# A transformer block on one core: q and k of three heads from unnormalised x, head 0's v and gate by seven products

## The chip, the cores and the metric

The kernel runs on one core of a Trainium2 chip. Five engines work beside each other, each through its own instructions in order: TensorE (PE; its weight loads are shown as PEld), VectorE (DVE), ScalarE (ACT), GpSimd (POOL) and SyncE (SP). DMAs are issued from a queue of SP, ACT or POOL. The metric is the time of one execution on the device in microseconds (us); smaller is better.

## The reference, cut to what matters

One encoder layer for 512 tokens of width 1024, in float32. The columns of `w_in` are [conv x | conv B | conv C | q | k | v | swish gate | gate A | gate R].

```python
def rmsnorm(x, g):
    xf = x.astype(jnp.float32)
    y = xf * lax.rsqrt(jnp.mean(xf * xf, axis=-1, keepdims=True) + EPS)
    return (y * g.astype(jnp.float32)).astype(x.dtype)
...
        h = rmsnorm(x, g_mix[l])
        proj = h @ w_in[l]
        xc, gb, gc, q, k, v, g_sw, gate_a, gate_r = jnp.split(proj, split_points, axis=-1)
...
        qf = rotary(q.reshape(b, s, RET_HEADS, RET_QK_DIM).astype(jnp.float32)) * (RET_QK_DIM ** -0.5)
        kf = rotary(k.reshape(b, s, RET_HEADS, RET_QK_DIM).astype(jnp.float32))
        vf = v.reshape(b, s, RET_HEADS, RET_V_DIM).astype(jnp.float32)
...
        ret_f = retention_chunkwise(qf, kf, vf, lg_f, strict=False)
        ret_b = jnp.flip(retention_chunkwise(jnp.flip(qf, 2), jnp.flip(kf, 2), jnp.flip(vf, 2),
                                             lg_b, strict=True), 2)
...
        y_r = (ret.astype(dt) * jax.nn.silu(g_sw)) @ w_r_out[l]
        merged = jax.nn.sigmoid(gate_a) * y_a + jax.nn.sigmoid(gate_r) * y_r
        x = x + merged @ w_o[l]
        h2 = rmsnorm(x, g_ffn[l])
        x = x + (jax.nn.silu(h2 @ w_ff_gate[l]) * (h2 @ w_ff_up[l])) @ w_ff_down[l]
    return rmsnorm(x, g_final)
```

There are four heads; q and k of a head are 256 wide, v and its swish gate 512. The retention weight of a pair of tokens is a power of a forward or a backward decay, by their distance.

## The kernel before, in words

**Precision.** Every matmul of the reference is made of three: each operand is split into a rounded part `hi` and a remainder `lo`, and `hi*hi + hi*lo + lo*hi` is summed in a bank (`mm3`, L282 to L286, and the inner loops of `prod`, L325, and `prod_tm`, L369). The split is a cast on ACT (L171, or L174 with a scale) and a subtraction on VectorE (L172 or L175).

**Weights.** A list written out by hand, `plan()`, gives the order in which weights are used. A block ("c") is loaded as 1 MB in two halves (L208) and split. A form of a quad ("q") comes from quarters of a pair of matrices (loaded at L232), some of them summed first on VectorE (L244), and is then split. `take()` hands out the next weights and prepares up to two units (`AHEAD`) more.

**Quads.** `strassen` (L379) makes two products that share their left side by seven half products instead of eight, `a11, s1, s2, a12, s3, a22, s4`, from sums of quarters of the activations (`sums`, L597) and of the weights. Some products add into a bank that a copy on ACT (`snap`, L376) has just read. A quad is 7 x 24 = 168 matmuls of 128x512.

**Start.** Eight small matmuls keep TensorE busy. Then `prefetch(4, load_x, split_x)` loads pieces of the first weight block and of x in turn, all from SP's queue, with the small columns `cols` ahead of x (L431, L432). `split_x` scales x by the gain `g_mix` and splits it into `xu`: this is x without its 1/rms. `SumSq` sums the squares; `rstd_tokens` (L470) gives 1/rms by token (a power on POOL, L482), and `rstd_row` (L490) the same as a row on all partitions, by two matmuls (L493, L494).

**Head 0's v and gate.** They are made first from `xu` by two plain products (`token_major`, L301), 96 matmuls each. Their eviction (L576) multiplies by 1/rms. `rstd_row` is asked for between the two products. Then x is normalised (L587) and split into `xg`, and the sums for the quads follow (L607).

**Order after that.** For each head: the quad of v and gate (not for head 0), then q and k from `xg` (`do_qk`, 96 matmuls of 128x512) with the rotation on VectorE out of the banks. Then two quads for the gates A and R, then the decay tables (`decays`), then the conv mixer, which is the first work after this stage with 256-wide products (L325). Everything is stored to DRAM from POOL's queue (`store`, L566) and loaded again later. The order of instructions on each engine is set when the kernel is built, by a scheduler that takes the program's order as priority and fills gaps with later work that is ready. So the decay tables, last in the program, stand within the first quad on the chip.

**End.** The last two products of the FFN's last part give the output in four blocks of tokens. `ev` adds a block to y (`to_y`, L1087 on VectorE, the square on ACT, L1089), scales and stores the block before it (`put`, L1111 on VectorE, or L1109 on ACT), and forms 1/rms of its own block (`rms`, L1097 and a power on POOL, L1099).

Pools: `big` has 14 tiles of 128x2048, `tmp` 9 of 128x512 (`t512`), `misc` 2, PSUM 8 banks.

Of the kernel before, what the change touches and what calls it, by code (L numbers as in the profile page):

```python
# [17 lines left out]
P = 128  # L18
D = 1024
# [25 lines left out]
AHEAD = 2  # L45
LEAD = 4

WIDTH = {"w": 512, "x": 256, "a": 512, "f": 256, "d": 512}  # L50
# [5 lines left out]
def plan():  # L56
# [16 lines left out]
            for u in (0, 2):  # L73
                out.append(("q", ("w", c0, c1), name, u, 2))

    for c in (C_V, C_G):
        for r in (0, 512):
            b("w_in", r, 4, c, 512)
    for h in range(HEADS):
        if h:  # L80
            quad(C_V + h * VD, C_G + h * VD)
        a("w_in", C_Q + h * QK)
        a("w_in", C_K + h * QK)
    for c in (0, 512):
        quad(C_GA + c, C_GR + c)
    for c0, c1 in ((C_XC, C_GC), (C_XC + 256, C_GC + 256), (C_GB, C_GB + 256)):
# [56 lines left out]
def block_kernel(ctx: ExitStack, tc: tile.TileContext, xT, xtok, wpack, wquad, cols, decs, rot, g_ffn, g_final, out):  # L143
# [284 lines left out]

    def load_x(k, n=1):
        if k == 0:  # L430
            nc.sync.dma_start(cols_sb, cols)  # L431
        nc.sync.dma_start(xs[k // 4][:, k % 4:k % 4 + n, :], xT[:, k:k + n, :])  # L432

    def split_x(k):
        split(xs[k // 4][:, k % 4, :], xu[0][k // 4][:, k % 4, :], xu[1][k // 4][:, k % 4, :],
# [15 lines left out]
    class SumSq:  # L451
# [18 lines left out]
        def rstd_tokens(self):  # L470

            ps = bank()
            for nb in range(NB):
                sl = slice(nb * P, (nb + 1) * P)
                nc.tensor.matmul(ps[:, 2 * nb:2 * nb + 2], self.hi[:, sl], ones_r[:, 0:2], start=True, stop=False)
                nc.tensor.matmul(ps[:, 2 * nb:2 * nb + 2], self.lo[:, sl], ones_r[:, 0:2], start=False, stop=True)
            r = small.tile([P, NB], F32, tag="rtok", name="rtok", bufs=2)
            v = small.tile([P, NB], F32, tag="rtokv", name="rtokv", bufs=2)
            nc.vector.tensor_scalar(
                out=v, in0=ps[:, 0:2 * NB].rearrange("p (n two) -> p n two", two=2)[:, :, 0],  # L480
                scalar1=1.0 / D, scalar2=EPS, op0=ALU.mult, op1=ALU.add)
            nc.gpsimd.tensor_tensor(out=r, in0=v, in1=mhalf[:, 0:NB], op=ALU.pow)  # L482
# [5 lines left out]
            return r  # L488

        def rstd_row(self):  # L490

# [6 lines left out]
    for k in range(8):  # L498
        ss.add(xs[k // 4][:, k % 4, :])
    ss.split()  # L500


    dec = const.tile([P, 8], F32, name="dec")
# [20 lines left out]

    nc.vector.tensor_scalar_mul(lgam[:, 4:8], lgam[:, 4:8], -1.0)


    def decays():
        delta_i = big.tile([P, 896], mybir.dt.int32, tag="big", name="delta_i", padded_shape=[P, 2048])
        nc.gpsimd.iota(delta_i, pattern=[[1, 896]], base=-384, channel_multiplier=-1)  # L530
        delta = big.tile([P, 896], F32, tag="big", name="delta", padded_shape=[P, 2048])
        nc.vector.tensor_copy(delta, delta_i)
        for h in range(HEADS):
            scr = big.tile([P, 896], F32, tag="big", name="scr", padded_shape=[P, 2048])
            tab = misctile(896, "tab")
            nc.vector.tensor_scalar(out=scr, in0=delta, scalar1=0.0, scalar2=lgam[:, 4 + h:5 + h],
                                    op0=ALU.min, op1=ALU.mult)
            nc.vector.tensor_scalar(out=tab, in0=delta, scalar1=0.0, scalar2=lgam[:, h:h + 1],
                                    op0=ALU.max, op1=ALU.mult)
            nc.vector.tensor_tensor(out=scr, in0=scr, in1=tab, op=ALU.add)  # L540
            nc.scalar.activation(tab, scr, AF.Exp)
            nc.sync.dma_start(tabs[h], tab)

    def kept(name):
        return dram.tile([P, 4, 512], F32, name=name)

    tabs = [dram.tile([P, 896], F32, name=f"tab{h}") for h in range(HEADS)]
    qkd = [(kept(f"qh{h}"), kept(f"ql{h}")) for h in range(HEADS)]  # L550
    vd = [kept(f"v{h}") for h in range(HEADS)]
    sgd = [kept(f"sg{h}") for h in range(HEADS)]
    gad = [kept(f"ga{j}") for j in range(2)]
    grd = [kept(f"gr{j}") for j in range(2)]

    zd = [[dram.tile([P, n, 4, 256], F32, name=f"z{i}{n}{j}") for i in range(2)]
          for j, n in enumerate((2, 2, 2, 1))]

    def keep(dst, src):
        hi, lo = t512(F32R), t512(F32R)  # L560
        split(src, hi, lo)
        for d, t in zip(dst, (hi, lo)):
            store(d, t.bitcast(F32))

    def store(dst, t):
        nc.gpsimd.dma_start(dst, t)  # L566


    def before_v(kk):
        if kk == 7:  # L570
            rtok.append(ss.rstd_tokens())
    rtok = []
# [11 lines left out]
    xg = quarters()  # L584
    for k in range(8):
        xk = xs[k // 4][:, k % 4, :]
        nc.vector.scalar_tensor_tensor(out=xk, in0=xk, scalar=gmix[:, k:k + 1], in1=rrow,  # L587
                                       op0=ALU.mult, op1=ALU.mult)
    for i in range(2):
        for k in (0, 2):  # L590
            split(xs[i][:, k:k + 2, :], xg[0][i][:, k:k + 2, :], xg[1][i][:, k:k + 2, :])

    def form_tile():
        t = big.tile([P, 2, 4, 256], F32R, tag="big", name="xform", padded_shape=[P, 2, 4, 256])
        return t[:, 0], t[:, 1]

    def sums(a11, a12, a21, a22):  # L597
        out = {}
        for name, o, in0, in1, op in (
                ("s1", a22, a21, a22, ALU.subtract), ("s3", a21, a11, a21, ALU.subtract),  # L600
                ("s2", a11, a22, a11, ALU.subtract), ("s4", a12, a12, a11, ALU.add)):
            nc.vector.tensor_tensor(out=o, in0=in0, in1=in1, op=op)
            out[name] = form_tile()
            split(o, *out[name])
        return out

    xf = sums(*(xs[i][:, :, o:o + 256] for o in (0, 256) for i in range(2)))  # L607
    for n, i, o in (("a11", 0, 0), ("a12", 1, 0), ("a22", 1, 256)):
        xf[n] = tuple(t[i][:, :, o:o + 256] for t in xg)
    xforms = {n: of(t) for n, t in xf.items()}  # L610

    def do_qk(h):
        for j in range(2):
            pss = []
            feature_major(xg, lambda m, ps: pss.append(ps))
            cos, sin = rcs[:, 0, :], rcs[:, 1, :]
            for i, (c1, c2, op) in enumerate(((cos, sin, ALU.subtract), (sin, cos, ALU.add))):
                a, b = t512(), t512()
                nc.vector.tensor_tensor(out=a, in0=pss[0], in1=c1, op=ALU.mult)
                nc.vector.tensor_tensor(out=b, in0=pss[1], in1=c2, op=ALU.mult)  # L620
                nc.vector.tensor_tensor(out=a, in0=a, in1=b, op=op)
                keep([t[:, 2 * j + i, :] for t in qkd[h]], a)
# [24 lines left out]

    def conv(m, b, u, c):
# [435 lines left out]
    def to_y(ps, nb, half):  # L1084

        yt, ac, i = y[half][:, nb, :], acs[nb], done[nb]
        nc.vector.tensor_tensor(out=yt, in0=ps, in1=yt, op=ALU.add)  # L1087
        sq = t512()
        nc.scalar.activation(sq, yt, AF.Square, accum_out=ac[:, i:i + 1])  # L1089
# [3 lines left out]
        done[nb] += 1  # L1093

    def rms(nb):
        ac = acs[nb]
# [55 lines left out]
def pack_weights(arrays):  # L1152
    out = np.empty((len(BLOCKS), P, CH), np.float32)
    for i, (_, name, row, nk, col, ncol) in enumerate(BLOCKS):
        blk = arrays[name][row:row + nk * P, col:col + ncol]
        out[i] = blk.reshape(nk, P, ncol).transpose(1, 0, 2).reshape(P, CH)
    return out

# [58 lines left out]
```

## Time and profile before

| what | value |
|---|---|
| median of 3 runs | 1043.47 us (1043.3 to 1043.92) |
| the profiled execution's own time | 1043.97 us |
| its span, first to last instruction | 1042.2 us |
| granted TensorE clock | 0.998 |
| VectorE busy / ACT busy / POOL busy | 84% / 50% / 10% of the span |
| DMA | 175.07 MB, mean 168 GB/s |

A line of the timeline reads: start in us from the span's start, duration, engine, line of the kernel, operation, what it writes and reads, shapes, count, and in brackets how long the engine had been idle and what ended that. A line of the chain of work reads: start, duration, engine and line, count. A line of groups gives busy time and the mean of one in ns behind the first bar, and idle time ahead of it behind the second. Starts are the measure for a stream of matmuls, since their ends are modelled and overlap.

### The profile page before, as it was taken

How to read it: one execution, taken by the hardware profiler on the slowest of the kernel's cores; microseconds unless marked ns; L12 is line 12 of the kernel's file. 1: busy time of each engine (PE TensorE's matmuls, PEld its weight loads, DVE VectorE, ACT ScalarE, POOL GpSimd, SP SyncE). 2: the span in 40 equal slices, each digit the busy share in tenths (PEclk: the TensorE clock that was granted, in tenths of full speed). 3: DMA queues.
4: the chain of work that ended last, by engine and by line, in shares of the span. 5: the costliest groups of instructions: out<-in, count | busy, mean ns of one | idle time of the engine just before them, and what ended most of it. 6: DMA issues, size and time to landing. Idle time of an engine off the chain costs nothing.

```text
span 1042.2 us, 14832 instructions
## 1 busy us (share of the span) xinstructions
PE 1028.3 (99%) x5664; PEld 897.0 (86%) x5664; DVE 875.5 (84%) x1127; ACT 523.4 (50%) x698; POOL 107.7 (10%) x180
## 2 busy tenths in 40 slices
PE   8999999999999999999999999999999999999996
PEld 7788888888888998888888888889998999899985
DVE  6999786858787888697989998669998899889995
ACT  6546745452656545243443234355555565556553
POOL 0121111111111004202011000000002000110011
PEclk9999999999999999999999999999999999999999
DMA  9635638173645576919176535630319322663322
GB/s 325 223 117 201 236 123 281 71 254 119 199 141 182 169 284 233 341 42 358 42 283 247 205 111 173 236 113 28 92 45 275 117 85 78 193 152 102 122 35 87
DMA packets 49688, 175.07 MB, mean 168 GB/s; under 512 B 6480, under 2 KB 6480, under 8 KB 46288
## 3 DMA queue, kind: packets, MB, share of 16 engines
q1 hardware_dynamic: 36592, 131.12, 36.9%
q0 software_dynamic: 13024, 43.00, 12.9%
q8 instruction: 44, 0.72, 0.3%
q14 instruction: 28, 0.23, 0.1%
HBM read 135.56 MB, written 38.54 MB: 167 GB/s over the span
## 4 chain that ended last, share of the span: by engine, by line
PE 77%; issue 9%; DVE 7%; DMA 3%; POOL 2%; ACT 1%; SPq 0%; POOLq 0%; DVEq 0%; ACTq 0%
PE bank L369 29%; PE bank L325 27%; PE bank L285 7%; PE bank L284 7%; PE bank L286 7%; DVE wlo L172 1%; POOL z L566 1%; DVE big L185 1%; DMA big<-ql 1%; DMA big<-xT 1%; DMA z<-t 1%; DMA tab<-tab 0%; DVE big L172 0%; DVE t L464 0%; DVE big L175 0%
## 5 line engine op out<-in xcount | busy, mean ns | idle before, releaser
L171 ACT CAST whi<-raw 128x1024 fp32r<-128x1024 f32 (+1 forms) x281 | 288.6, 1032 | 302.7 <-PE bank L369 66.4
L172 DVE TENSOR_TENSOR wlo<-raw,whi 128x1024 fp32r<-128x1024 f32 (+1 forms) x281 | 335.8, 1202 | 108.8 <-ACT whi L171 107.8
L325 PE MATMUL bank<-xform,whi 128*128 128x256 f32 x1440 | 260.3, 283 | 0.0
L325 PEld LDWEIGHTS bank<-xform,whi 128*128 128x128 f32 x1440 | 224.8, 192 | 0.7 <-ACT t L376 0.6
L325 PE MATMUL bank<-xform,wlo 128*128 128x256 f32 x720 | 203.7, 283 | 0.0
L369 PE MATMUL bank<-whi,big 128*128 128x512 f32 x548 | 172.4, 390 | 0.0
L244 DVE TENSOR_TENSOR raw<-raw 128x1024 f32<-128x1024 f32 (+1 forms) x124 | 148.5, 1205 | 1.8 <-DMA raw<-wquad 0.4
L325 PEld LDWEIGHTS bank<-xform,wlo 128*128 128x128 f32 x720 | 138.2, 192 | 0.0
L369 PEld LDWEIGHTS bank<-whi,big 128*128 128x128 f32 x548 | 102.7, 188 | 22.4 <-DVE big L172 0.6
L369 PE MATMUL bank<-wlo,big 128*128 128x512 f32 x274 | 106.7, 389 | 0.0
L369 PE MATMUL bank<-whi,xform 128*128 128x512 f32 x320 | 101.2, 389 | 0.3 <-ACT t L376 0.3
L284 PE MATMUL bank<-whi,big 128*128 128x512 f32 x240 | 94.3, 395 | 1.8 <-ACT big L174 1.8
L285 PE MATMUL bank<-wlo,big 128*128 128x512 f32 x240 | 94.3, 393 | 0.0
L286 PE MATMUL bank<-whi,big 128*128 128x512 f32 x240 | 93.4, 392 | 0.0
L284 PE MATMUL bank<-big,whi 128*128 128x512 f32 x224 | 87.1, 389 | 0.0
L285 PE MATMUL bank<-big,whi 128*128 128x512 f32 x224 | 87.1, 389 | 0.0
L286 PE MATMUL bank<-big,wlo 128*128 128x512 f32 x224 | 87.1, 389 | 0.0
L376 ACT COPY t<-bank 128x512 f32<-128x512 f32 x96 | 55.5, 585 | 35.8 <-PE bank L369 17.2
L369 PEld LDWEIGHTS bank<-whi,xform 128*128 128x128 f32 x320 | 60.1, 188 | 13.1 <-ACT t L376 0.7
L369 PE MATMUL bank<-wlo,xform 128*128 128x512 f32 x160 | 62.2, 389 | 0.0
L369 PEld LDWEIGHTS bank<-wlo,big 128*128 128x128 f32 x274 | 51.4, 188 | 10.5
L284 PEld LDWEIGHTS bank<-whi,big 128*128 128x128 f32 x240 | 45.5, 190 | 12.5 <-ACT big L174 2.1
(173 smaller groups left out, 1398.6 us busy)
## 6 DMA issues: line engine op xcount, KB each, us to landing
raw<-wquad SPq DMA_DIRECT2D x124, 512.0 KB, 4.4
raw<-wpack SPq DMA_DIRECT2D x58, 512.0 KB, 4.9
z<-t POOLq DMA_DIRECT2D x24, 256.0 KB, 4.9
zform<-z POOLq DMA_DIRECT2D x6, 1024.0 KB, 6.2
v<-t POOLq DMA_DIRECT2D x16, 256.0 KB, 5.0
sg<-t POOLq DMA_DIRECT2D x16, 256.0 KB, 3.3
qh<-t POOLq DMA_DIRECT2D x16, 256.0 KB, 2.6
ql<-t POOLq DMA_DIRECT2D x16, 256.0 KB, 2.7
```

What stands on the lines that cost most here:

```text
L171: nc.scalar.copy(hi, src)
L172: nc.vector.tensor_tensor(out=lo, in0=src, in1=hi.bitcast(F32), op=ALU.subtract)
L185: nc.vector.transpose(o[:, :, :, b, :], i[:, :, :, q, :])
L244: nc.vector.tensor_tensor(out=t, in0=t, in1=raws[quad, more, u][:, 0:n], op=ALU.add)
L284: nc.tensor.matmul(ps, lh, rh, start=first, stop=False)
L285: nc.tensor.matmul(ps, lh, rl, start=False, stop=False)
L286: nc.tensor.matmul(ps, ll, rh, start=False, stop=last)
L325: nc.tensor.matmul(o, l[:, c], r[:, k], start=start and s == 0 and k == 0 and i == 0, stop=stop and k == 3 and i == 2, skip_group_check=True)
L369: nc.tensor.matmul(pss[tt], l, r[:, c], start=start and k == 0 and i == 0, stop=stop and k == n - 1 and i == 2, skip_group_check=True)
L376: nc.scalar.copy(t, ps)
L566: nc.gpsimd.dma_start(dst, t)
```

## The change

- `plan()` starts with six blocks, for each of three heads (`EARLY`) the columns of q and k side by side; head 0's v and gate become a quad as the others are.
- The first products are now q and k of heads 0 to 2 from `xu`, 96 matmuls a head, into four banks, which ACT copies into a `big` tile each. `rstd_tokens` goes ahead of step 7 of head 0's product, `rstd_row` ahead of step 1 of head 1's, and the normalisation of x and its splits after it.
- The rotation of these q and k takes a table of cosines and sines that is multiplied by the row of 1/rms (`rcn`). The six rotations are held back, one for each quad (`turn_one`).
- `decays()` makes the tables in two halves of 448 columns, each entry as the product of two exponentials, in `t512` tiles, right after head 0's quad in the program. Their stores go from SP's queue to POOL's.
- x is loaded from ACT's queue, `cols` from POOL's.
- At the end, `put` of the block before is ordered behind the new block's sum on VectorE and behind its square on ACT.

```diff
+EARLY = 3
...
-    for c in (C_V, C_G):
+    for h in range(EARLY):
         for r in (0, 512):
-            b("w_in", r, 4, c, 512)
+            b("w_in", r, 4, (C_Q + h * QK, C_K + h * QK), 512)
     for h in range(HEADS):
-        if h:
-            quad(C_V + h * VD, C_G + h * VD)
-        a("w_in", C_Q + h * QK)
-        a("w_in", C_K + h * QK)
+        quad(C_V + h * VD, C_G + h * VD)
+        if h >= EARLY:
+            a("w_in", C_Q + h * QK)
+            a("w_in", C_K + h * QK)
...
         if k == 0:
-            nc.sync.dma_start(cols_sb, cols)
-        nc.sync.dma_start(xs[k // 4][:, k % 4:k % 4 + n, :], xT[:, k:k + n, :])
+            nc.gpsimd.dma_start(cols_sb, cols)
+        nc.scalar.dma_start(xs[k // 4][:, k % 4:k % 4 + n, :], xT[:, k:k + n, :])
...
+    def decays():
+        for o in (0, 448):
+            delta = t512(mybir.dt.int32)[:, 0:448]
+            nc.gpsimd.iota(delta, pattern=[[1, 448]], base=o - 384, channel_multiplier=-1)
+            ahead, behind = (t512()[:, 0:448] for _ in range(2))
+            nc.vector.tensor_scalar(out=ahead, in0=delta, scalar1=0.0, scalar2=None, op0=ALU.max)
+            nc.vector.tensor_scalar(out=behind, in0=delta, scalar1=0.0, scalar2=None, op0=ALU.min)
+            for h in range(HEADS):
+                f, g = (t512()[:, 0:448] for _ in range(2))
+                nc.scalar.activation(f, ahead, AF.Exp, scale=lgam[:, h:h + 1])
+                nc.scalar.activation(g, behind, AF.Exp, scale=lgam[:, 4 + h:5 + h])
+                nc.vector.tensor_tensor(out=f, in0=f, in1=g, op=ALU.mult)
+                store(tabs[h][:, o:o + 448], f)
...
+    early = []
+    for h in range(EARLY):
+        pss = [bank() for _ in range(4)]
+        for kk in range(8):
+            if kk % 4 == 0:
+                c = Chunk()
+            if (h, kk) == (0, 7):
+                ss.rstd_tokens()
+            if (h, kk) == (1, 1):
+                rrow = snap(ss.rstd_row())
+
+                xg = quarters()
...
+            for m in range(4):
+                mm3(pss[m], c.w(kk % 4, m * P, P), act_pair(xu, kk), kk == 0, kk == 7)
+        t = bigtile()
+        for m in range(4):
+            nc.scalar.copy(t[:, m, :], pss[m])
+        early.append(t)
...
-    for dst, func in ((vd[0], AF.Copy), (sgd[0], AF.Silu)):
-        def ev(nb, ps):
-            t = t512()
-            nc.scalar.activation(t, ps, func, scale=rtok[0][:, nb:nb + 1])
-            store(dst[:, nb, :], t)
-        token_major(xu, 0, 2, ev, None if rtok else before_v)
-        if func == AF.Copy:
-            rrow = snap(ss.rstd_row())
...
+    rcn = misctile(D, "rcn").rearrange("p (i n) -> p i n", i=2)
     for i in range(2):
+        nc.vector.tensor_tensor(out=rcn[:, i, :], in0=rcs[:, i, :], in1=rrow, op=ALU.mult)
+    held = [(h, j) for h in range(EARLY) for j in range(2)]
+
+    def turn_one():
+
+        if held:
+            h, j = held.pop(0)
+            rotate(h, j, early[h][:, 2 * j, :], early[h][:, 2 * j + 1, :], rcn)
...
             store(left[:, 2 + tt, :], t)
+            if tt:
+                turn_one()
...
     for h in range(HEADS):
-        if h:
-            do_quad(vd[h], sgd[h], AF.Silu)
-        do_qk(h)
+        do_quad(vd[h], sgd[h], AF.Silu)
+        if h == 0:
+            decays()
+        if h >= EARLY:
+            do_qk(h)
     for j in range(2):
         do_quad(gad[j], grd[j], AF.Sigmoid, AF.Sigmoid)
-    decays()
+    while held:
+        turn_one()
...
     def ev(ps, nb, half):
-        to_y(ps, nb, half)
+        add, square = to_y(ps, nb, half)
         if held:
-            put(held.pop())
+            with tc.issue_after(add.ins), tc.issue_after(square.ins):
+                put(held.pop())
         else:
             gain(0, 0)
             gain(1, 0)
```

More of the change, by code (lines that the diff above doesn't have):

```diff
@@ new lines, in kept @@
+    def kept(name):
+        return dram.tile([P, 4, 512], F32, name=name)
+    tabs = [dram.tile([P, 896], F32, name=f"tab{h}") for h in range(HEADS)]
+    qkd = [(kept(f"qh{h}"), kept(f"ql{h}")) for h in range(HEADS)]
+    vd = [kept(f"v{h}") for h in range(HEADS)]
+    sgd = [kept(f"sg{h}") for h in range(HEADS)]
+    gad = [kept(f"ga{j}") for j in range(2)]
+    grd = [kept(f"gr{j}") for j in range(2)]
+    zd = [[dram.tile([P, n, 4, 256], F32, name=f"z{i}{n}{j}") for i in range(2)]
+          for j, n in enumerate((2, 2, 2, 1))]
@@ new lines, in keep, with store @@
+    def keep(dst, src):
+        hi, lo = t512(F32R), t512(F32R)
+        split(src, hi, lo)
+        for d, t in zip(dst, (hi, lo)):
+            store(d, t.bitcast(F32))
+    def store(dst, t):
+        nc.gpsimd.dma_start(dst, t)
+    rrow = None
+    early = []
[9 more added lines that the diff above has]
+                xg = quarters()
+                for k in range(8):
+                    xk = xs[k // 4][:, k % 4, :]
+                    nc.vector.scalar_tensor_tensor(out=xk, in0=xk, scalar=gmix[:, k:k + 1], in1=rrow,
+                                                   op0=ALU.mult, op1=ALU.mult)
+                for i in range(2):
+                    for k in (0, 2):
+                        split(xs[i][:, k:k + 2, :], xg[0][i][:, k:k + 2, :], xg[1][i][:, k:k + 2, :])
+            for m in range(4):
[4 more added lines that the diff above has]
+        early.append(t)
@@ new lines, in form_tile, with sums @@
+    def form_tile():
+        t = big.tile([P, 2, 4, 256], F32R, tag="big", name="xform", padded_shape=[P, 2, 4, 256])
+        return t[:, 0], t[:, 1]
+    def sums(a11, a12, a21, a22):
+        out = {}
+        for name, o, in0, in1, op in (
+                ("s1", a22, a21, a22, ALU.subtract), ("s3", a21, a11, a21, ALU.subtract),
+                ("s2", a11, a22, a11, ALU.subtract), ("s4", a12, a12, a11, ALU.add)):
+            nc.vector.tensor_tensor(out=o, in0=in0, in1=in1, op=op)
+            out[name] = form_tile()
+            split(o, *out[name])
+        return out
@@ L503, in block_kernel @@
+    xf = sums(*(xs[i][:, :, o:o + 256] for o in (0, 256) for i in range(2)))
+    for n, i, o in (("a11", 0, 0), ("a12", 1, 0), ("a22", 1, 256)):
+        xf[n] = tuple(t[i][:, :, o:o + 256] for t in xg)
+    xforms = {n: of(t) for n, t in xf.items()}
     dec = const.tile([P, 8], F32, name="dec")
@@ L525, in block_kernel @@
     nc.vector.tensor_scalar_mul(lgam[:, 4:8], lgam[:, 4:8], -1.0)
[L528 to L542, printed above, removed]
@@ L597, in sums @@
[L597 to L607, printed above, removed]
@@ L608, in block_kernel, with rotate @@
-    for n, i, o in (("a11", 0, 0), ("a12", 1, 0), ("a22", 1, 256)):
-        xf[n] = tuple(t[i][:, :, o:o + 256] for t in xg)
-    xforms = {n: of(t) for n, t in xf.items()}
+    def rotate(h, j, t1, t2, table):
+        cos, sin = table[:, 0, :], table[:, 1, :]
+        for i, (c1, c2, op) in enumerate(((cos, sin, ALU.subtract), (sin, cos, ALU.add))):
+            a, b = t512(), t512()
+            nc.vector.tensor_tensor(out=a, in0=t1, in1=c1, op=ALU.mult)
+            nc.vector.tensor_tensor(out=b, in0=t2, in1=c2, op=ALU.mult)
+            nc.vector.tensor_tensor(out=a, in0=a, in1=b, op=op)
+            keep([t[:, 2 * j + i, :] for t in qkd[h]], a)
@@ L615, in do_qk @@
             feature_major(xg, lambda m, ps: pss.append(ps))
[L616 to L622, printed above, removed]
+            rotate(h, j, *pss, rcs)
     def do_quad(left, right, func, func_left=None):
```

40 lines of the change are left out of this document (5 added, 35 removed).

## The prediction

> **What bounds the kernel now.** I read the page first, then what TensorE waited for, then the busy time by stage, then the chain of work and single stretches of the timeline.
>
> ```profile
> span 1042.2 us, 14832 instructions
> ## 1 busy us (share of the span) xinstructions
> PE 1028.3 (99%) x5664; PEld 897.0 (86%) x5664; DVE 875.5 (84%) x1127; ACT 523.4 (50%) x698; POOL 107.7 (10%) x180
> ```
>
> The profiled execution took 1043.97 us for this span, 0.50 over the median of 1043.47. TensorE is busy for 99% of it, so I ask two things of every edit: does it remove matmuls, and does it make TensorE wait. These are its waits in the first 120 us, longest first, and the busy time by stage (the first quad product starts at 78, the last product of the gates ends at 334):
>
> ```profile
> PE bank L284 <- ACT big L174: 1.8, 1, 1.8
> PE bank L493 <- ACT t L171: 1.7, 1, 1.7
> ```
>
> ```profile
> core 0: us, PE busy (x) PEld busy (x) DVE busy (x) ACT busy (x) POOL busy (x), PEclk, DMA share, GB/s
> 0.00:78.00 78.00, 73.34 (x315) 60.16 (x316) 66.08 (x106) 44.08 (x59) 11.02 (x22) 1.00 0.63 221
> 50.00:80.00 30.00, 30.00 (x134) 24.85 (x133) 29.59 (x32) 14.83 (x17) 5.23 (x9) 1.00 0.30 106
> 78.00:334.00 256.00, 255.70 (x1128) 211.38 (x1127) 199.45 (x217) 138.08 (x169) 35.87 (x66) 1.00 0.54 183
> 334.00:1042.00 708.00, 699.28 (x4224) 625.47 (x4222) 610.01 (x805) 341.28 (x471) 60.82 (x92) 1.00 0.47 157
> ```
>
> The reader is to see that from 78 to 334 TensorE lacks 0.3 us of 256, and that VectorE is the second engine. In 50 to 80 it is busy for 29.59 of 30 us and TensorE still loses nothing. The price of a matmul comes from the chain of work, where the two gate quads stand as one piece:
>
> ```profile
> 258.10 76.21 PE bank L369 x336
> ```
>
> 76.21 / 336 = 0.2268 us for one 512-wide matmul, and the last gate quad ends at 334.3.
>
> **Products.** Head 0's v and gate go from two plain products, 2 x 8 x 4 x 3 = 192 matmuls, to seven half products of 2 x 4 x 3 = 24, that is 168. q and k keep 2 x 2 x 8 x 3 = 96 a head in either form. So 24 matmuls go: 24 x 0.2268 = **-5.4 us**. They lie on the engine that is 99% busy, and nothing but a new wait can give them back. Ahead of the first quad stand 192 + 96 = 288 matmuls before and 3 x 96 = 288 after, so the sums and splits of x have the same cover as now.
>
> **The wait for the row of 1/rms.** Before, the row is asked for right after the v product:
>
> ```profile
> 30.41 1.02 POOL L482 TENSOR_TENSOR rtok<-rtokv,mhalf 128x4 f32<-128x4 f32 x1 [5.75 <-DVE lw L517]
> ```
>
> ```profile
> 31.21 0.39 PE L286 MATMUL bank<-whi,big 128*128 128x512 f32 x1
> 33.33 0.50 PE L493 MATMUL bank<-t,ones_r 128*128 128x512 f32 x1 [1.72 <-ACT t L171]
> ```
>
> The two starts are 2.12 us apart where 0.23 would do: 1.9 us lost, plus 0.2 before the second half (a guess). After, the sums still go in ahead of step 7 of the first product, but the row is asked for after step 0 of the next one: 24 matmuls (5.4 us) behind them where there were 12 (2.7 us). The chain was 1.9 late and gets 2.7 more. The decay logarithm, whose small VectorE steps (L517) sit between the links of this chain, now comes later in the program. I take **-2.1**, bounds -2.3 and 0. Next late would be the copying out of the first product's four banks (4 ACT copies of 0.59, row below), which has 12 matmuls of cover; ACT is free for 34 of the first 78 us.
>
> **x on ACT's queue, the columns on POOL's.** The start, first SP's issues, then ACT's instructions, then TensorE:
>
> ```profile
> 0.73 0.39 SPq L208 DMA_DIRECT2D raw<-wpack  x1
> 1.17 0.42 SPq L431 DMA_DIRECT2D cols_sb<-cols  x1
> 1.64 0.42 SPq L432 DMA_DIRECT2D big<-xT  x1
> ...
> 4.48 3.32 SPq L432 DMA_DIRECT2D big<-xT  x3
> ```
>
> ```profile
> 4.18 0.62 ACT L171 CAST whi<-raw 128x512 fp32r<-128x512 f32 x1 [1.86 <-DMA raw<-wpack]
> 5.90 0.72 ACT L174 ACTIVATE big<-big,cols_sb 128x512 fp32r<-128x512 f32 x1 [1.10 <-DMA big<-xT]
> ```
>
> ```profile
> 6.67 0.79 PE L284 MATMUL bank<-whi,big 128*128 128x512 f32 x1 [1.85 <-ACT big L174]
> ```
>
> The first matmul waits for x's first load, issued third. It can go 1.64 - 0.73 = 0.91 us earlier: the best end. Against it, the last three x loads held SP's queue until 7.80. If they hold ACT's queue as long, the cast at 4.18 and the scaling at 5.90 stand behind them: 7.80 + 0.62 + 0.72 = 9.14, 2.5 us later: the worst end. Every matmul follows, so either counts in full. ACT's queue will carry the six x loads alone, without the weight and column loads that SP had in flight, so I take a value near the good end, **-0.2**. The columns go to a POOL that works 11 of 78 us. I price their move at nothing: their cover is x's own landing, and if they land after it the loss lies within the same bounds.
>
> **VectorE and ACT under the quads.** The stage from the first quad to the last now holds six quads and one q/k: 6 x 168 + 96 = 1104 matmuls, 250.3 us. VectorE's prices, from its groups in 78 to 334 and two stretches of its timeline:
>
> ```profile
> L172 DVE TENSOR_TENSOR wlo<-raw,whi 128x1024 fp32r<-128x1024 f32 x81 | 98.9, 1223 | 45.1 <-ACT whi L171 44.8
> L244 DVE TENSOR_TENSOR raw<-raw 128x1024 f32<-128x1024 f32 x38 | 46.2, 1222 | 0.4
> ```
>
> ```profile
> 44.85 4.63 DVE L172 TENSOR_TENSOR big<-big 128x1024 fp32r<-128x1024 f32 x4
> ...
> 71.51 0.68 DVE L619 TENSOR_TENSOR t<-bank,rcs 128x512 f32<-128x512 f32 x1
> 72.11 0.68 DVE L620 TENSOR_TENSOR t<-bank,rcs 128x512 f32<-128x512 f32 x1
> ```
>
> Back to back, a 1024-wide one takes (4.63 - 1.22) / 3 = 1.14, a 512-wide one 72.11 - 71.51 = 0.60. A quad has 14 splits, 8 weight sums and 6 result sums: 22 x 1.14 + 6 x 0.60 = 28.7. With one held rotation (8 x 0.60 = 4.8) it is 33.5 of its 38.1 us. Six make 201. Head 3's q/k adds 4 x 1.14 + 16 x 0.60 = 14.2, the decays 12 x at most 0.60 = 7.2, at 512-wide prices for 448 columns. Together **222.6 of 250.3 us, 89%**, where the stage stood at 199.45 of 256 (78%). It fits, and 50 to 80 shows that 98% can fit, so I price the rotations, the sums and the two products for the normalised table at nothing. Their cover is these 28 us of slack.
>
> ACT carries what can disturb TensorE. After the product s3 its bank is copied out (L376) and the product a22 writes the same bank. The first bank's copy has six matmuls, 1.36 us, of cover. The decays now issue 16 exponentials inside the first quads:
>
> ```profile
> 94.33 0.59 ACT L376 COPY t<-bank 128x512 f32<-128x512 f32 x1 [0.73 <-PE bank L369]
> 94.81 1.05 ACT L171 CAST whi<-raw 128x1024 fp32r<-128x1024 f32 x1
> 95.88 1.28 ACT L541 ACT_TABLE_LOAD   x1
> 97.17 0.96 ACT L541 ACTIVATE tab<-scr 128x896 f32<-128x896 f32 x1
> ```
>
> A table load ahead of such a copy costs TensorE 1.28 + 0.59 - 1.36 = 0.5 us; a load with an exponential behind it 1.47. The bounds are 0 and 4 x 1.47 = 5.9. I take two loads, **+1.0**, because ACT is half idle and its order already leaves room ahead of the copies (idle 0.73 in the first row). The table stores go to POOL, eight instead of SP's four, on an engine busy for 36 of 256 us. What waits behind them are stores of v and gates, which nobody reads before the scores.
>
> **The end.** VectorE's last instructions, and the last matmul:
>
> ```profile
> 1031.17 1.42 DVE L1111 SCALAR_TENSOR_TENSOR big<-big,fin,gf 128x512 f32<-128x512 f32 x2 [0.66 <-POOL fin L1099]
> 1032.50 0.69 DVE L1087 TENSOR_TENSOR big<-bank,big 128x512 f32<-128x512 f32 x1
> 1033.98 0.16 DVE L1097 SCALAR_TENSOR_TENSOR fin<-fin 128x1 f32<-128x1 f32 x1 [0.79 <-ACT t L1089]
> 1034.79 0.75 DVE L1111 SCALAR_TENSOR_TENSOR big<-big,fin,gf 128x512 f32<-128x512 f32 x1 [0.65 <-POOL fin L1099]
> 1035.46 0.68 DVE L1087 TENSOR_TENSOR big<-bank,big 128x512 f32<-128x512 f32 x1
> 1036.93 0.16 DVE L1097 SCALAR_TENSOR_TENSOR fin<-fin 128x1 f32<-128x1 f32 x1 [0.79 <-ACT t L1089]
> 1037.75 0.75 DVE L1111 SCALAR_TENSOR_TENSOR big<-big,fin,gf 128x512 f32<-128x512 f32 x1 [0.66 <-POOL fin L1099]
> ```
>
> ```profile
> 1033.33 0.39 PE L369 MATMUL bank<-whi,big 128*128 128x512 f32 x1
> ```
>
> The last bank is ready at 1033.72, but its sum (L1087) starts at 1035.46, behind the scaling of the block before it. With that scaling ordered behind the sum and behind the square, the sum starts at about 1033.75 and the rest of the chain (2.29 to the last scaling, then the store) follows unchanged: **-1.7**, bounds -1.8 and 0. The sum before it has room too: its bank is full 12 matmuls earlier, at 1031.0, and the pair of scalings then ends by about 1033.1. What is queued behind the new order is the earlier block's scaling. It leaves at about 1035.9 at the latest, still before the last block's.
>
> **Sum**: -5.4 - 2.1 - 0.2 - 1.7 + 1.0 = -8.4 us. Against the profiled execution that is 1043.97 - 8.4 = 1035.6, on the median **1035.1**.
>
> **Rivals.** (1) The x loads hold ACT's queue: +2.5 in place of -0.2, 1037.8. For it: the 3.32 us row. Against it: a queue of its own. (2) The copies come late in the first quads: +5.9 in place of +1.0, 1040.0. For it: 16 exponentials and their table loads among copies with 1.36 us of cover. Against it: the stage before held four exponentials and their table loads (one at 95.88), and TensorE lost 0.3 us in all of it. (3) A change of table costs more than its load, say ACT stands empty for another 1.28: two copies are late by 1.8 each, 3.6 in place of 1.0, 1037.7. The exponential at 97.17 starts 0.01 us after its load, which speaks against it. The Trainium skill (ScalarE: Activation LUTs, What ACT_TABLE_LOAD costs) gives about 1283 ns for the load and 1380 ns for a drain at each switch to another set; by its figures this estimate would be 1037.9, and the trace agrees with the first figure and shows no room for the second. (4) **Slower: VectorE becomes the bound in the quads.** It waited 45.1 us there for ACT's casts. If these waits can't be squeezed they come on top of its work: 222.6 + 45.1 = 267.7 against 250.3, +17.4, 1052.5. The result is slower than before from 38 us of surviving waits on (222.6 + 38.2 = 250.3 + 10.5) and about equal from 34 on. For it: the rotations are moved into the stage where VectorE was the second engine. Against it: 50 to 80. (5) The start and the end do nothing: 1035.1 + 0.2 + 1.7 = 1037.0, inside the forecast's own range.
>
> **How the numbers follow.** A difference of 0.2% (2.1 us) is about what can be told from no change here. Forecast 0.54, its own range 1031.5 (all best ends: -5.4 - 2.3 - 0.9 - 1.8 = -10.4 gives 1033.1; 1.6 more if the rest of TensorE's idle time in the first stage goes too, 78 - 73.34 = 4.7 us, of which 3.0 are in the sum's best ends) to 1037; (1) 0.14; (2) 0.12; (3) 0.02; (4) slower 0.10, and at a lesser strength, no difference, 0.08. So faster 0.82, same 0.08, slower 0.10. The range runs from 1031.5 to 1040.5, past (2), and leaves out (4).
>
> **What would show it.** Right: 5640 matmuls; the first one near 6.5; no wait over 0.5 us at L493; the first 256-wide product (L325) near 326 instead of 334.3; the last sum within 0.1 us of the last matmul, and 6.8 instead of 8.5 us from the last matmul's end to the span's end. Wrong: a first matmul after 8; TensorE waiting for L376 or for L172 between 75 and 326; VectorE near 100% there.

## The result: slower, and the profile after

| | median us | range of the runs |
|---|---|---|
| before | 1043.57 | 1043.3 to 1043.92 |
| after | 1050.03 | 1049.7 to 1053.46 |

After takes 1.0069 times as long by the means of the runs, with a 95% interval of 1.0055 to 1.0082: 7.2 us slower (6.5 us between the medians), where 8.4 us faster was forecast. The profiled execution of after took 1050.1 us. The page after, its first lines:

```profile
span 1048.3 us, 14824 instructions
...
PE 1026.1 (98%) x5640; PEld 894.8 (85%) x5640; DVE 890.9 (85%) x1148; ACT 537.1 (51%) x728; POOL 113.3 (11%) x190
```

The 24 matmuls are gone (5640 for 5664), and TensorE is busy for less time (1026.1 for 1028.3 us) in a longer span, so it waits more. What it waited for, in the whole span (total, times, longest; lines have moved by two, L325 is now L327, L369 is L371, L171 is L173):

```profile
PE bank L371 <- ACT whi L173: 4.9, 1, 4.9
PE bank L286 <- ACT big L176: 3.7, 1, 3.7
PE bank L477 <- ACT t L173: 2.8, 1, 2.8
PE bank L371 <- DVE wlo L174: 1.8, 1, 1.8
...
PE bank L494 <- ACT t L173: 0.9, 1, 0.9
```

Busy time by stage, with the columns of the table in the prediction (PE, its weight loads, DVE, ACT, POOL, then the granted clock):

```profile
0.00:82.00 82.00, 73.55 (x314) 60.43 (x315) 58.28 (x95) 39.07 (x54) 4.19 (x10) 0.96 0.48 174
82.00:121.00 39.00, 39.00 (x174) 32.31 (x173) 29.07 (x29) 25.58 (x32) 3.37 (x7) 1.00 0.46 149
121.00:145.00 24.00, 17.28 (x64) 13.28 (x63) 23.22 (x31) 18.05 (x27) 8.61 (x16) 0.79 0.45 165
145.00:342.00 197.00, 197.00 (x871) 163.07 (x870) 167.18 (x184) 112.28 (x143) 34.07 (x63) 1.00 0.57 198
```

Two stretches carry the loss: the first 82 us, and 24 us around the start of head 1's quad. There 64 matmuls ran where 24 / 0.2268 = 106 have room: 42 x 0.2268 = 9.5 us lost. From 145 to 342, where five rotations and head 3's q and k lie, TensorE lost nothing.

To set the account up I take starts of TensorE's instructions: the first quad product, the first 256-wide product, the last matmul. The first fence is before, the second after:

```profile
77.81 0.39 PE L369 MATMUL bank<-whi,big 128*128 128x512 f32 x1
334.14 0.40 PE L325 MATMUL bank<-big,whi 128*128 128x256 f32 x2
```

```profile
82.12 0.39 PE L371 MATMUL bank<-whi,big 128*128 128x512 f32 x1
...
342.42 0.40 PE L327 MATMUL bank<-big,whi 128*128 128x256 f32 x2
...
1040.84 0.39 PE L371 MATMUL bank<-whi,big 128*128 128x512 f32 x1
```

| stretch | before | after | difference |
|---|---|---|---|
| to the first quad product | 77.81 | 82.12 | +4.31 |
| quads and gates | 256.33 | 260.30 | +3.97 |
| conv mixer to the last matmul (1033.33 before) | 699.19 | 698.42 | -0.77 |
| last matmul's end to the span's end | 8.48 | 7.07 | -1.41 |
| span | 1042.2 | 1048.3 | +6.1 |

The row of the quads holds the loss of 9.5 us at head 1 and the gain of the 24 missing matmuls: 9.5 - 5.4 = 4.1, against 3.97.

**The first 82 us.** ScalarE's instructions and its queue's DMAs (ACTq) in after:

```profile
5.38 0.34 ACTq L434 DMA_DIRECT2D big<-xT  x1
...
7.43 0.72 ACT L176 ACTIVATE big<-big,cols_sb 128x512 fp32r<-128x512 f32 x1 [1.06 <-DMA cols_sb<-cols]
...
12.23 0.72 ACT L176 ACTIVATE big<-big,cols_sb 128x512 fp32r<-128x512 f32 x1 [1.31 <-DMA big<-xT]
12.24 0.84 ACTq L434 DMA_DIRECT2D big<-xT  x2
...
19.15 1.34 ACT L176 ACTIVATE big<-big,cols_sb 128x512 fp32r<-128x512 f32 x2 [4.99 <-DMA big<-xT]
21.72 1.34 ACT L176 ACTIVATE big<-big,cols_sb 128x512 fp32r<-128x512 f32 x2 [1.23 <-DMA big<-xT]
23.90 0.62 ACT L461 ACTIVATE t<-big 128x512 f32<-128x512 f32 x1
```

The last two loads of x leave at 12.24, the moment the scaling of x's fourth block has started: in ScalarE's order they stand behind it, and that scaling waited for the load before. Before, from SyncE's queue, they had all left by 7.80. So x's second half is there at 19 to 22 us. The squares (L461) begin at 23.90, all eight behind the last scaling. In run 1 below, with x on SyncE's queue, they stand between the scalings from 7.18 on, and the last one starts at 19.61:

```profile
7.18 0.62 ACT L461 ACTIVATE t<-big 128x512 f32<-128x512 f32 x1
```

So the squares are late by the late loads and by their order on ScalarE. No run parts the two, but both go with x's queue (run 10). The matmul of the token sums (L477), ahead of which TensorE stood 2.81 us, comes at 35.88 instead of 27.8.

**The block of exponentials.** ScalarE around 130 us, and TensorE there:

```profile
127.31 1.05 ACT L173 CAST whi<-raw 128x1024 fp32r<-128x1024 f32 x1 [2.32 <-DVE raw L246]
128.37 1.28 ACT L514 ACT_TABLE_LOAD   x1
129.67 0.67 ACT L514 ACTIVATE t<-t,lgam 128x448 f32<-128x448 f32 x1
...
134.16 1.98 ACT L173 CAST whi<-raw 128x1024 fp32r<-128x1024 f32 x2
136.11 0.67 ACT L514 ACTIVATE t<-t,lgam 128x448 f32<-128x448 f32 x1
```

```profile
130.86 0.39 PE L371 MATMUL bank<-whi,xform 128*128 128x512 f32 x1
136.19 1.22 PE L371 MATMUL bank<-whi,big 128*128 128x512 f32 x2 [4.95 <-ACT whi L173]
139.18 0.80 PE L371 MATMUL bank<-wlo,big 128*128 128x512 f32 x1 [1.77 <-DVE wlo L174]
```

Eight exponentials stand without a gap from 129.67 to 134.16, then two casts of weights, then eight more exponentials. TensorE waits for the second of these casts (the pair ends at 136.14). Before, four exponentials stood singly between casts from 97.2 to 126.3 and TensorE lost 0.3 us in that whole stage.

### The profile page after: what moved, and what is told of

Read it like the earlier page. It is cut to its first block, busy times and chain, and to the rows that moved or that the text cites. A ratio compares the mean times of both kernels' runs of the same rounds, so it can differ in the third digit from the quotient of the medians.

```text
span 1048.3 us, 14824 instructions
## 1 busy us (share of the span) xinstructions
PE 1026.1 (98%) x5640; PEld 894.8 (85%) x5640; DVE 890.9 (85%) x1148; ACT 537.1 (51%) x728; POOL 113.3 (11%) x190
## 4 chain that ended last, share of the span: by engine, by line
PE 92%; DVE 3%; DMA 2%; issue 1%; ACT 0%; POOL 0%; POOLq 0%; DVEq 0%; ACTq 0%
PE bank L371 33%; PE bank L327 27%; PE bank L286 10%; PE bank L287 10%; PE bank L288 10%; DMA big<-xT 2%; DVE wlo L174 1%; DVE t L466 0%; DVE raw L246 0%; PE bank L935 0%; PE bank L886 0%; ACT whi L173 0%; DMA raw<-wquad 0%; DVE t L516 0%; DVE big L1137 0%
## 5 line engine op out<-in xcount | busy, mean ns | idle before, releaser
L173 ACT CAST whi<-raw 128x1024 fp32r<-128x1024 f32 (+1 forms) x287 | 293.1, 1032 | 295.6 <-PE bank L371 67.4
L174 DVE TENSOR_TENSOR wlo<-raw,whi 128x1024 fp32r<-128x1024 f32 (+1 forms) x287 | 340.5, 1199 | 96.9 <-ACT whi L173 95.2
L327 PE MATMUL bank<-xform,whi 128*128 128x256 f32 x1440 | 260.3, 283 | 0.0
L327 PEld LDWEIGHTS bank<-xform,whi 128*128 128x128 f32 x1440 | 224.8, 192 | 0.7 <-ACT t L378 0.5
L327 PE MATMUL bank<-xform,wlo 128*128 128x256 f32 x720 | 203.7, 283 | 0.0
L371 PE MATMUL bank<-whi,big 128*128 128x512 f32 x596 | 189.3, 393 | 4.9 <-ACT whi L173 4.9
L246 DVE TENSOR_TENSOR raw<-raw 128x1024 f32<-128x1024 f32 (+1 forms) x132 | 157.2, 1202 | 3.2 <-DMA raw<-wquad 1.9
L327 PEld LDWEIGHTS bank<-xform,wlo 128*128 128x128 f32 x720 | 138.2, 192 | 0.0
L371 PEld LDWEIGHTS bank<-whi,big 128*128 128x128 f32 x596 | 112.6, 189 | 29.7 <-ACT whi L173 5.4
L371 PE MATMUL bank<-whi,xform 128*128 128x512 f32 x384 | 121.5, 390 | 0.0
L371 PE MATMUL bank<-wlo,big 128*128 128x512 f32 x298 | 117.2, 393 | 1.8 <-DVE wlo L174 1.8
L378 ACT COPY t<-bank 128x512 f32<-128x512 f32 x102 | 59.3, 586 | 53.3 <-PE bank L371 25.5
L371 PEld LDWEIGHTS bank<-whi,xform 128*128 128x128 f32 x384 | 72.4, 188 | 15.1
L371 PE MATMUL bank<-wlo,xform 128*128 128x512 f32 x192 | 74.9, 390 | 0.0
L286 PE MATMUL bank<-whi,big 128*128 128x512 f32 x176 | 68.9, 392 | 0.0
L287 PE MATMUL bank<-wlo,big 128*128 128x512 f32 x176 | 68.5, 389 | 0.0
L371 PEld LDWEIGHTS bank<-wlo,big 128*128 128x128 f32 x298 | 56.5, 190 | 14.1 <-DVE wlo L174 2.5
L288 PE MATMUL bank<-whi,big 128*128 128x512 f32 x176 | 68.1, 390 | 0.0
L286 PEld LDWEIGHTS bank<-big,whi 128*128 128x128 f32 x224 | 42.6, 191 | 12.7 <-ACT big L176 3.9
```

The lines of the kernel that those rows point to most:

```text
L173: nc.scalar.copy(hi, src)
L174: nc.vector.tensor_tensor(out=lo, in0=src, in1=hi.bitcast(F32), op=ALU.subtract)
L246: nc.vector.tensor_tensor(out=t, in0=t, in1=raws[quad, more, u][:, 0:n], op=ALU.add)
L286: nc.tensor.matmul(ps, lh, rh, start=first, stop=False)
L287: nc.tensor.matmul(ps, lh, rl, start=False, stop=False)
L288: nc.tensor.matmul(ps, ll, rh, start=False, stop=last)
```

## Experiments

Medians of before beside them: 1042.98 (runs 1 to 4), 1043.36 (5 to 8), 1043.17 (9 to 12).

**1. x and the columns from SyncE's queue again.**

```diff
-            nc.gpsimd.dma_start(cols_sb, cols)
-        nc.scalar.dma_start(xs[k // 4]..., xT...)
+            nc.sync.dma_start(cols_sb, cols)
+        nc.sync.dma_start(xs[k // 4]..., xT...)
```

> The changed kernel with x and the columns loaded from SP's queue again, as before. Theory A: the two queues cost the start. The columns landed at 7.41 instead of 4.34 and held the first scaling, and the last x loads, issued on ACT at 12.2 and 12.6, came in at 19.1 and 21.7 and made the sums of squares late. Then the first matmul is back at 6.7, the wait ahead of the sums for 1/rms (2.97 us) is gone, the first quad starts near 75.7 instead of 82.3, and the time is 1050.0 - 6.6 = 1043.4. Rival: the early products cost the start themselves (q and k against x in two parts need ACT's copies and the same sums of squares), the queues only 1.5 us of first matmul: first quad near 80.8, time 1048.5. The wait near 131 stays in both.

Measured 1042.91, ratio to before 0.9997 (0.9988 to 1.0006): 7.1 us less than after. Its three longest waits:

```profile
PE bank L371 <- ACT whi L173: 5.0, 1, 5.0
PE bank L286 <- ACT big L176: 2.8, 1, 2.8
PE bank L371 <- DVE wlo L174: 1.8, 1, 1.8
```

The waits at L477 and L494 are gone, and the first quad product starts at 75.73, 2.1 us ahead of before. The two waits at head 1's quad are nearly unchanged (5.0 and 1.8 us). So the queues cost 7 us, and the loss at head 1 has another cause.

**2. The decays called behind the gates** (`decays()` moved from the loop over heads to just ahead of `while held`).

> The changed kernel with the call that makes the decay tables behind the gate quads in the program, as before. Theory B: the wait of about 9.9 us between 130.9 and 144 comes from eight exponentials with a table load that stand on ACT ahead of the casts of head 1's first weights. Then the wait is gone or under 1 us, and the time is 1050.0 - 9.5 = 1040.5. Rival C: VectorE is full there (23.2 of 24 us busy between 121 and 145) because of the rotation in head 0's quad, and the decays only happen to be near: the wait stays at 5 us or more, 1045 or above.

Measured 1054.27, ratio 1.0102 (1.0088 to 1.0116). **3. Both edits together.**

> Both of these edits together: loads on SP's queue and the decay tables last. If the two losses are separate (theories A and B) they add: 1050.0 - 6.6 - 9.5 = 1033.9, that is about 9.7 us under the kernel before (5.4 of products, 2.1 of the row of 1/rms, 1.4 of the end, 0.8 elsewhere). If one hides the other, the time is nearer to the lower of the two single ones, 1040.

Measured 1045.88, ratio 1.0026 (1.0016 to 1.0036). Both expectations failed: the loss moved along with the decays. The longest wait of run 3, and half of its exponentials (the other eight are on L515; duration min/median/max in ns, first and last start):

```profile
PE bank L327 <- ACT t L378: 10.3, 1, 10.3
```

```profile
L514 ACT ACTIVATE t<-t,lgam x8: 652/653/668, 333.1 to 342.0; 128x448 f32<-128x448 f32 x8
```

The two blocks now stand at the start of the conv mixer, and a bank's copy (L378) behind them keeps TensorE for 10.3 us. Head 1's quad, with all rotations still in place, lost nothing (108 matmuls in the 24 us from 115). So the rotations alone don't make the loss, and a later call alone is no cure.

**4. The kernel before with the ordered end alone** (the last part of the diff, nothing else).

> The kernel before with the ordered end alone. From the last matmul's end to the span's end it took 8.5 us before and 7.1 in the changed kernel. If the order does that by itself: 1043.5 - 1.4 = 1042.1, last sum within 0.1 us of the last matmul. If the shorter end came with the other edits: 1043.5.

Measured 1042.21, ratio 0.9988 (0.998 to 0.9997), between 0.3 and 2.1 us faster. The forecast of 1.7 lies within that.

**5. As run 1, with the old decays** (one exponential of 128x896 a head) behind the gates, their tables in `big` tiles.

```diff
-                f, g = (t512()[:, 0:448] for _ in range(2))
...
+            tab = big.tile([P, 896], F32, tag="big", ...)
+            nc.scalar.activation(tab, scr, AF.Exp)
```

> The changed kernel with three parts undone: x and the columns loaded from SyncE's queue again, and the decays in their old form (one Exp of 128x896 a head, four Exps) called behind all the gates, as before; their table is held in a tile of the big pool, because both misc tiles are still taken, and GpSimd's queue stores it. What stays: the early products of q and k, the seven products for all v and gates, and the ordered end. Theory R (the ring of nine t512 tiles: the new decays take 22 of them in program order, so the copies of the next product wait until the Exps are done; tiles of another pool leave the Exps free to be put singly into ScalarE's gaps): no wait of TensorE above 2.5 us between 75 and 340 us, and 1033.5 (1042.9 of the run with x and columns on SyncE, less the 9.8 us of stall). Rival W (ScalarE and VectorE have no room for decays and rotations in the stage of quads, whatever the tiles): the stall is spread over more and shorter waits, 1038 or more.

Measured 1038.05, ratio 0.9957 (0.9944 to 0.9969). Between 75 and 340 us no wait is longer than 2.1 us, as theory R said, but the time is 4.6 us above its 1033.5.

**6. As run 3, with `big` tiles for the new decays instead of `t512`.**

```diff
-            ahead, behind = (t512()[:, 0:448] for _ in range(2))
+            ahead, behind = (big.tile([P, 448], F32, tag="big", ...) for _ in range(2))
```

> x and the columns from SyncE's queue again; the decays in the new form (two powers by halves, sixteen Exps of 128x448 and eight products) called behind all the gates, with their tiles from the big pool instead of the ring of t512 tiles. Theory R: no stall of 10 us at the start of any stage; sixteen Exps cost TensorE at most 1.5 us more than four, through five more table loads of 1.28 us on ScalarE, 1033.5 to 1035. Rival F (the form, sixteen Exps and eight products, is what costs): the stall of about 9.8 us is there in another place or spread, 1040 or more.

Measured **1037.14** (1035.26 to 1038.92), ratio 0.994 (0.9927 to 0.9952): faster than both kernels by more than the measurement's uncertainty, and 5.8 us under run 1. It is still 2.1 us above the upper end that theory R gave. Its waits, the longest two, and half of its exponentials:

```profile
PE bank L371 <- ACT t L378: 2.5, 2, 1.6
PE bank L286 <- ACT big L176: 1.4, 1, 1.4
```

```profile
L514 ACT ACTIVATE half<-half,lgam x8: 654/668/672, 89.0 to 269.5; 128x448 f32<-128x448 f32 x8
```

Sixteen exponentials and eight products are still there, in the same place of the program as in run 3. They now stand singly over 180 us. ScalarE even loads a table 13 times in this stage, while TensorE's waits for it come to 2.5 us:

```profile
L649 ACT ACT_TABLE_LOAD x7 | 9.0, 1283 | 0.1
L515 ACT ACT_TABLE_LOAD x3 | 3.8, 1283 | 0.1
L514 ACT ACT_TABLE_LOAD x3 | 3.8, 1283 | 0.1
```

So the form is not what costs; run 5, with the old form, is no faster.

**7. As run 1 (decays behind head 0's quad), with `big` tiles.**

> x and the columns from SyncE's queue again; the decays in the new form and in their new place, behind the first head's quad, but with their tiles from the big pool instead of the ring of t512 tiles: only the tiles differ from the run with x and the columns on SyncE, which took 1042.9. Theory R: the Exps are no longer two blocks of eight, the 5 us wait at the start of the second head's quad is gone, 1033.5 to 1036. Rival P (place: sixteen Exps ahead of the second head's casts in the program's order hold ScalarE there): the stall stays, 1042 to 1043.

Measured 1042.75, ratio 0.9992 (0.9984 to 1.0001). The block at head 1 is gone (24 us of it, first row, with 107 matmuls), but 30 us in the next head lose nearly as much (94 matmuls where 132 have room, 38 x 0.2268 = 8.6 us, second row):

```profile
115.00:139.00 24.00, 24.00 (x107) 19.84 (x107) 22.76 (x23) 14.14 (x17) 3.24 (x6) 1.00 0.51 170
176.00:206.00 30.00, 25.24 (x94) 19.20 (x93) 21.21 (x27) 23.06 (x30) 8.01 (x15) 0.89 0.60 205
```

Runs 1, 7, 3 and 6 differ in just two things, the tiles and the place in the program (times against before):

| | `t512`, ring of 9 | `big`, pool of 14 |
|---|---|---|
| called behind head 0's quad | 0.9997 | 0.9992 |
| called behind the gates | 1.0026 | **0.994** |

Neither change helps alone. A likely reading: called early, the exponentials stand ahead of the casts of later heads in the scheduler's priority. Called late but in the ring of `t512`, they can't be pulled forward, since every tile they take comes after those of the gates. The table shows the two effects; this reading of them is argued and not shown, from where the blocks stood (129.67 in after, 333.1 in run 3, spread from 89.0 in run 6). Both theories of runs 5 to 7 (ring, place) were half right.

**8. After, without the rotation in head 0's quad** (made behind the gates).

> The changed kernel without the rotation of the first head's first half in the first head's quad; it is made behind the gates instead, with the one left over. Theory R: the block of Exps and the wait behind it stay, 1049 to 1050.5. Rival V (VectorE, which was busy without a gap from 113 to 141 us, is late because of the rotation at 116 to 126 us, six operations of 0.68 us and four splits): the wait at 131 to 139 us shrinks by at least 4 us, 1046 or less.

Measured 1055.24, ratio 1.0116 (1.0103 to 1.0129). This is above both forecasts. The waits of 4.9 and 1.8 us in the quads became 2.7 (two) and 1.3 (two), and from 121 to 145 us 78 matmuls ran for 64, so VectorE's load does count there. But two rotations now stand at the mixer's start, and a wait of 4.9 us there is new:

```profile
PE bank L327 <- ACT t L378: 4.9, 1, 4.9
...
PE bank L371 <- ACT whi L173: 2.7, 2, 2.3
```

**9. Only the columns back on SyncE's queue.**

> The changed kernel with only the columns back on SyncE's queue; x stays on ScalarE's. Theory S (both queues cost: the columns on GpSimd's queue hold the first product, 8.20 against 6.67 us, with fourteen slow matmuls against eight; x on ScalarE's queue holds the 1/rms row, waits of 2.97 and 1.04 us): the first wait gets shorter and the waits of 2.97 and 1.04 us stay, 1047.3 (1050.0 less 1.5 and 1.2). Rival X (x alone costs, the columns would have come in time): 1050.

Measured 1050.59, ratio 1.0074 (1.0061 to 1.0087). **10. Only x back.**

> The changed kernel with only x back on SyncE's queue; the columns stay on GpSimd's. Theory S: the first product still waits for the columns to about 8 us, the waits at 30 to 40 us are gone, 1046 (1050.0 less 2.97 and 1.04). Rival K (the columns alone cost, and the late last loads of x would be hidden): 1050.

Measured 1043.11, ratio 0.9998 (0.999 to 1.0007). x alone makes the whole 7 us; the columns cost nothing, though the first scaling in after did wait 1.06 us for them. With the columns back the first matmul went from 8.20 to 7.02 us, the wait at L477 grew to 3.49 us, and the first quad product came at 82.44 for 82.12: the earlier start gained nothing. The wait at L477 took 0.68 of its 1.18 us back; where the rest went was not traced.

**11. The decays without the exponentials. 12. Without VectorE's products.**

> The changed kernel whose decays leave out the sixteen Exps (the product of the two halves of the index is stored instead, still made by VectorE in tiles of the ring). Theory E (the block of Exps stands on ScalarE ahead of the casts of the second head's weights): the wait of 4.9 us and the slow matmuls behind it at 131 to 139 us are gone, 1040 to 1042. Rival V (VectorE, without a gap from 113 to 141 us, would be late without the Exps too): a wait of 3 us or more stays there, 1045 or more.

> The changed kernel whose decays leave out the eight products of VectorE (the second Exp writes the tile that is stored; the sixteen Exps stay). Theory E: the wait behind the block of Exps stays, 1048.5 to 1050. Rival V: VectorE is 8 times 0.61 us freer there, the wait shrinks by 4 us or more, 1046 or less.

Run 11 measured 1046.4, ratio 1.0038 (1.0024 to 1.0051; its profiled execution, 1050.41, was the longest of its runs); run 12 1051.92, ratio 1.0085 (1.0071 to 1.01). Run 11's longest wait in the quads, then run 12's, and the 24 us from 121 in each:

```profile
PE bank L371 <- DVE wlo L174: 3.3, 1, 3.3
```

```profile
PE bank L371 <- ACT t L378: 8.0, 1, 8.0
```

```profile
121.00:145.00 24.00, 20.70 (x79) 16.37 (x78) 24.00 (x33) 10.37 (x13) 8.60 (x16) 0.86 0.40 148
```

```profile
121.00:145.00 24.00, 15.99 (x62) 12.80 (x61) 17.52 (x22) 18.89 (x29) 8.63 (x16) 0.79 0.38 142
```

Without exponentials VectorE (third figure) is full for the 24 us and a split comes late; without products it has 24 - 17.52 = 6.5 us to spare, and TensorE waits 8.0 us for a copy behind ScalarE's block. So a block on ScalarE is enough to make the loss without VectorE's products. But run 12's block is not after's: with no products between them, all sixteen exponentials stand in one piece from 130.92 to 139.97. Run 11 shows that without exponentials VectorE still makes a smaller loss (79 matmuls for 106, 27 x 0.2268 = 6.1 us in its longest execution), so the exponentials are not the whole of it.

## Why the prediction was wrong

- **Products, -5.4: right.** 5640 matmuls. In run 6 the stage from the first quad product (74.29) to the first 256-wide one (327.68) takes 253.39 us; 1104 x 0.2268 = 250.4, and its 2.5 us of waits make most of the other 3.0.
- **Row of 1/rms, -2.1: right in mechanism, undone by the next step.** With x on SyncE (runs 1, 6 and 10) TensorE no longer waits there, and in run 1 the first quad product comes 2.1 us ahead of before. In after the sums came too late, since x and its squares did.
- **x on ACT's queue, -0.2 with bounds of -0.9 and +2.5: the step that failed first.** It measured about +7 (1050.03 in after, 1043.11 in run 10). The step asked what the loads do to ScalarE's instructions ("they hold ACT's queue"), and whether the first product is late. It did not ask what ScalarE's instructions do to the loads: they leave in ScalarE's order, and two of six stood behind a scaling that waits for another. The bound took the first matmul alone. That came at 8.20, past the 8 that the prediction named as a sign of being wrong, but most of the price lay some 28 us later, at the sums of squares, and it undid this gain of the row too (first quad product at 82.12, with x on SyncE at 75.73, before at 77.81). Rival (1) named the queue and had the blocking the wrong way round, at about a third of the size.
- **The columns, at nothing: right.**
- **VectorE at 89%, at nothing: right for five of the six rotations** (145 to 342: 167.18 of 197 us busy, and no loss). The parts of its sum make 222.4 us and not 222.6, which changes nothing. What the average hid is the 24 us at head 1, where VectorE was busy for 23.22; runs 8 and 11 show it as a part of the loss there. That 50 to 80 ran at 98% without a loss did not carry over to this stretch. Rival (4), whose time of 1052.5 came near, did not happen: VectorE was no bound over the stage, and the nearness is chance.
- **Exponentials, +1.0 with bounds of 0 and 5.9: the second step that failed.** The stretch with the two blocks lost 9.5 us, past the upper bound, with VectorE's part in it. The tiles and the call alone are worth 5.8 us (run 1 against run 6). The term and its upper bound both took a late copy behind one exponential at a time, as before had them. The step counted work and engine time and not what the exponentials stand in line with: they came in blocks of eight, ahead of a cast of weights. That the ring of nine tiles and the early call made these blocks is the reading argued above.
- **The end, -1.7: right in mechanism, -1.4 in size.** The last sum starts within 0.1 us of the last matmul's end (1040.84 + 0.39), and the tail is 7.07 us for 8.48:

```profile
1041.27 0.69 DVE L1112 TENSOR_TENSOR big<-bank,big 128x512 f32<-128x512 f32 x1 [0.64 <-PE bank L371]
```

The terms that were right come to light in run 6, which undoes the two steps that failed: by the medians it is 6.2 us faster than before (1037.14 for 1043.36), where the sum said 8.4. Its profiled span is 8.8 us shorter (1033.4 for 1042.2), but that was its fastest execution, 1035.26, so the closeness to 8.4 proves nothing.

What stays open: why the early call with `big` tiles (run 7) loses nearly as much in another head. Its waits are for VectorE's splits (2.6 us) and a copy (1.8 us), and no run parted the two. How much of the loss at head 1 in after is ScalarE's and how much VectorE's is open as well.

## What to carry to other kernels

A load that is issued from a computing engine's queue leaves in that engine's order: look at what it stands behind there, and price it at the first place that needs the last byte, not the first. When filler work is moved, ask which pool its tiles come from and where its call stands in the program: here only the late call together with the larger pool got rid of the loss, and the sum of engine time says nothing of that. An average over a stage hides a short stretch in which an engine is full.

## What the runs showed of the hardware

TensorE's clock can fall after a short wait, and the wait then costs more than its length. In run 7 it fell after an idle time of 1.80 us, in run 6 it did not after 1.59 us. Length alone doesn't decide: in after the granted clock stayed at 1.00 from 35.80 to 38 us, behind the wait of 2.81 us. Run 7, then run 6:

```profile
180.55 0.57 PE L371 MATMUL bank<-whi,big 128*128 128x512 f32 x1 [1.80 <-ACT t L378]
...
181.35 1.05 PE L371 MATMUL bank<-whi,big 128*128 128x512 f32 x2
182.20 0.63 PE L371 MATMUL bank<-wlo,big 128*128 128x512 f32 x1
```

```profile
179.43 0.50 PE L371 MATMUL bank<-whi,big 128*128 128x512 f32 x1 [1.59 <-ACT t L378]
179.77 0.39 PE L371 MATMUL bank<-wlo,big 128*128 128x512 f32 x1
180.00 0.63 PE L371 MATMUL bank<-whi,big 128*128 128x512 f32 x2
```

In run 7 two matmuls take 182.20 - 181.35 = 0.85 us, 0.43 each, and this lasts to 183.9; in run 6 they keep 0.23. In after, behind the waits of 4.95 and 1.77 us, the granted clock between 139 and 144 us is 0.51, and 12 matmuls ran where 22 have room, 10 x 0.2268 = 2.3 us:

```profile
139.00:144.00 5.00, 4.82 (x12) 3.81 (x13) 4.25 (x7) 4.53 (x8) 1.62 (x3) 0.51 0.76 273
```

The Trainium skill (TensorE: Matmul & The Clock Gate, Part 1) gives half rate after at least one idle window of about 3.4 us, on a window that runs freely. The factor of a half agrees with 0.51, and the 4.95 us of after are longer than that window. The 1.80 us of run 7 are shorter, so there the measurement differs from the rule; what decides in such cases, no run here shows.
